# Two of the four weight sums of each seven-product step formed by accumulating DMA transfers, with six buffers for sums instead of four

## The chip, the core and the metric

The kernel runs on one core of one Trainium2 chip. The metric is the device time of one execution in microseconds (us). The core has five instruction streams that run in order, each on its own: TensorE (PE, matmuls), VectorE (DVE), ScalarE (ACT), GpSimd (POOL), and SyncE (SP), which here issues nearly all DMA transfers. They wait for one another by semaphores. An instruction that waits holds up everything behind it on its engine.

## The reference, cut to what matters

Two layers of a streaming encoder are applied to 592 tokens (16 learned meta tokens, 512 frames of a new stream, 64 frames of a running one) of width 1024:

```
def _swiglu(x, w_gate, w_up, w_down):
    return (jax.nn.silu(x @ w_gate) * (x @ w_up)) @ w_down
...
    for l in range(DEPTH):
        h = h + 0.5 * _swiglu(_rmsnorm(h, ln_ffa_w[l]), ffa_w_gate[l], ffa_w_up[l], ffa_w_down[l])
        m, c, s, g = _mixer(_rmsnorm(h, ln_mix_w[l]), ...)
        h = h + m
        h = h + 0.5 * _swiglu(_rmsnorm(h, ln_ffb_w[l]), ffb_w_gate[l], ffb_w_up[l], ffb_w_down[l])
    return _rmsnorm(h, ln_f_w), ...
```

The hidden width of each of the four feed-forward blocks (FFN) is 2816. The mixer is one input projection, a state-space scan and a gated linear attention side by side, and one output projection. All is float32. The change touches the gate and up products of the FFNs only.

## The kernel before

The activations stay in SBUF as `h`, 8 blocks of 128 features by 592 tokens. An FFN walks over 22 blocks of 128 hidden columns in four chunks (6, 6, 5 and 5 blocks). Within a chunk the gate and up products of its blocks come first, then eight down products that add into `h`.

The first two blocks of an FFN are multiplied in plain float32 (L593). Each of the other 20 is a `Quad`: the gate and the up weights of the block, each cut into an upper and a lower half of 512 rows (g1, g2, u1, u2), are replaced by seven matrices, so that seven products (in the order g1, s1, s2, s4, s3, g2, u2) do the work of eight half products. Four of the seven are sums of weights:

s1 = u1 + u2, s2 = s1 + g1, s4 = s2 + g2, s3 = g1 + u1.

Each of the seven matrices is then split by `convert` into a high part on ACT (tile `wh`, L542) and a low part on DVE (tile `wl`, L546). A product is 12 matmuls of 128x296 (L627 high by high, L628 high weights by low activations, L629 low by high). Results leave PSUM through the sink in `gated`: the sink of product s3 (L895, tile `u`) must be done before the last product, u2, may start, because they share an accumulator, and the next steps are L899, L906, L909 and L915 on DVE. So a Quad is 84 matmuls on PE, and there are 80 Quads in the program.

Weights arrive by SP, 256 KB a tile (128 partitions by 4 rows of 512 bytes), in `raw` buffers (tag `raw`, six of them, tile `wr`). The sums go into buffers with the tag `zq` (tile `ws`), which the mixers use too.

A planner fixes the order on every engine at build time: each step of the program is a generator that yields the engine and a planned duration, and the planner emits the step that could start first. The planned times only set the order; on the chip each engine takes its list from the top, and waits at its head for what is late.

Of the kernel before, what the change touches and what calls it, by code (L numbers as in the profile page):

```python
# [9 lines left out]
F32 = mybir.dt.float32  # L10
# [3 lines left out]
ALU = mybir.AluOpType  # L14
PSUM = bass.MemoryType.PSUM

P = 128
# [7 lines left out]
T = NMETA + SEQ + DEC  # L25
# [9 lines left out]


BLK = ((0, 128), (128, 128), (256, 128), (384, 128), (512, 80))
NT = 50
UK = 4
LEVELS = (64, 32, 16, 8, 4, 2, 1)  # L40

# [73 lines left out]
def ns_dve(n):  # L115
    return 67 + n / 0.96


def ns_act(n):
    return 90 + n / 1.2  # L120
# [76 lines left out]
def body(ctx: ExitStack, tc: tile.TileContext, a: dict, o: dict):  # L197
    nc = tc.nc
    V, S, G, PE, SP = nc.vector, nc.scalar, nc.gpsimd, nc.tensor, nc.sync

    const = ctx.enter_context(tc.tile_pool(name="const", bufs=1))
    res = ctx.enter_context(tc.tile_pool(name="res", bufs=1))
    sb = ctx.enter_context(tc.tile_pool(name="sb", bufs=1))
    ps = ctx.enter_context(tc.tile_pool(name="ps", bufs=1, space=PSUM))
    plan = Plan({PE: (200.0, 60.0), V: (220.0, 0.0), S: (265.0, 0.0), G: (100.0, 0.0)}, {G: V})
    bT = Buf(sb, "T", NT, [P, T], F32, 6)
    bhw = Buf(sb, "hw", 6, [P, HT], F32)
    bzq = Buf(sb, "zq", 4, [P, T], F32)
    braw = Buf(sb, "raw", 6, [P, UK, P], F32)
    bhi = Buf(sb, "whi", 6, [P, UK, P], F32R)  # L210
    blo = Buf(sb, "wlo", 6, [P, UK, P], F32R)
# [185 lines left out]
    def near(order):  # L397
        return 1e-3 * order
# [51 lines left out]
    def fetch():  # L450
# [9 lines left out]
        for i, job in enumerate(jobs):  # L460
            if isinstance(job, Quad):
                yield from fetch_quad(i, job, chain)
                continue
            src = job.src.rearrange("(k p) c -> p k c", p=P)
            for k0, k1, u in job.units:
                if job.whole:
                    if i == 0:
                        yield from whole(i, job, src, k0, k1, u, chain)
                    else:
                        plan.add(near(job.order), whole(i, job, src, k0, k1, u, chain))  # L470
                    if i == 0:
                        for b, g in ((0, 1), (1, 1), (2, 1)) if k0 == 0 else ():
                            yield from fetch_x(b, g)
                    continue
                t = yield "DMA", 190 * (k1 - k0), (), (braw,)
                raw = braw.tile(f"wr{i}", [P, k1 - k0, src.shape[2]])
                SP.dma_start(raw, src[:, k0:k1])
                t += 2000.0
                if job.few:
                    plan.add(near(job.order), convert_few(i, job, u, raw, t, chain))  # L480
                else:
                    plan.add(near(job.order), convert(u, raw, chain, braw.put, t))
            if i == 1:
                for b, g in ((3, 0), (4, 0), (3, 1), (4, 1)):
                    yield from fetch_x(b, g)
                t = yield "DMA", 380, ()
                SP.dma_start(cf[:, P:], a["c_f"][:, P:3 * P])
                cf_ev.set(t + 2000)
                load_params()
# [11 lines left out]
    def scaled(norm, k0, k1, u, t):  # L501
# [2 lines left out]
        V.tensor_tensor(u.hi[:, :u.n], u.hi[:, :u.n], w.to_broadcast([P, u.n, P]), op=ALU.mult)  # L504
        u.ready.set(t)

    def fetch_quad(i, job, chain):
        half = UK * P
        got = {}
        for name, w, r0 in (("g1", job.wg, 0), ("u1", job.wu, 0), ("u2", job.wu, half), ("g2", job.wg, half)):  # L510
            t = yield "DMA", 190 * UK, (), (braw,)
            raw = braw.tile(f"wr{i}")
            SP.dma_start(raw, w[r0:r0 + half].rearrange("(k p) c -> p k c", p=P))
            got[name] = [raw, Ev(), Ev({"g1": 3}.get(name, 2), braw.put)]
            got[name][1].set(t + 2000.0)
        for name, n in (("s1", 2), ("s2", 2), ("s4", 1), ("s3", 1)):
            got[name] = [None, Ev(), Ev(n, bzq.put)]
        plan.add(near(job.order), combine(i, got))
        for k, ((name, _, _), u) in enumerate(zip(QUAD, job.units)):
            raw, ev, use = got[name]  # L520
            plan.add(near(job.order + k), convert(u, got[name], chain, use.set, ev))

    def combine(i, got):
        for name, p, q in (("s1", "u1", "u2"), ("s2", "s1", "g1"), ("s4", "s2", "g2"), ("s3", "g1", "u1")):
            t = yield V, ns_dve(UK * P), (got[p][1], got[q][1]), (bzq,)
            dst = got[name][0] = bzq.tile(f"ws{i}", [P, UK, P])
            V.tensor_tensor(dst, got[p][0], got[q][0], op=ALU.add)  # L527
            got[name][1].set(t)
            got[p][2].set(t)
            got[q][2].set(t)  # L530

    def convert(u, raw, chain, done, *waits):

        prev, chain[0] = chain[0], Ev()
        split = chain[0]
        n = u.n * P
        t = yield S, ns_act(n), (*waits, prev) if prev else waits, (bhi,)
        if isinstance(raw, list):
            raw = raw[0]
        u.hi = bhi.tile("wh")  # L540
        hi = u.hi[:, :u.n]
        S.activation(hi, raw, AF.Copy)  # L542
        split.set(0.0)
        t = yield V, ns_dve(n), (t,), (blo,)
        u.lo = blo.tile("wl")
        V.tensor_tensor(u.lo[:, :u.n], raw, hi.bitcast(F32), op=ALU.subtract)  # L546
        done(t)
        u.ready.set(t)
# [145 lines left out]
    class Norm:  # L694
# [20 lines left out]
        def start(self):  # L715
            if self.first:
                self.first = False
                self.hi, self.lo, self.made = [None] * KD, [None] * KD, [Ev() for _ in range(KD)]
                self.rstd = res.tile([P, T], F32, tag="rstd", name=f"rs_{self.name}", bufs=2)
                plan.add(near(self.order), self.finish())  # L720

        def feed(self, m, hf, sl, *ts):
# [272 lines left out]
    for e in range(2):  # L995
        t = const.tile([P, 5 * P], F32, name=f"att{e}")
# [939 lines left out]
```

## Time and profile before

| | before |
|---|---|
| runs (us) | 2345.09, 2344.61, 2342.85 (median 2344.61) |
| profiled execution (us) | 2345.73, of which span 2343.6 |
| granted TensorE clock | 0.995 of full speed |
| busy: PE, DVE, ACT, POOL (us) | 2307.6, 1703.8, 1083.8, 122.0 |
| DMA, mean | 80 GB/s, 188 MB |

The span is the time from the first to the last instruction that the profile shows. The profiled execution is 1.1 us above the median of the runs; sums are made against the profiled one and then moved by that.

### The profile page before, as it was taken

How to read it: one execution, taken by the hardware profiler on the slowest of the kernel's cores; microseconds unless marked ns; L12 is line 12 of the kernel's file. 1: busy time of each engine (PE TensorE's matmuls, PEld its weight loads, DVE VectorE, ACT ScalarE, POOL GpSimd, SP SyncE). 2: the span in 40 equal slices, each digit the busy share in tenths (PEclk: the TensorE clock that was granted, in tenths of full speed). 3: DMA queues.
4: the chain of work that ended last, by engine and by line, in shares of the span. 5: the costliest groups of instructions: out<-in, count | busy, mean ns of one | idle time of the engine just before them, and what ended most of it. 6: DMA issues, size and time to landing. Idle time of an engine off the chain costs nothing.

```text
span 2343.6 us, 42925 instructions
## 1 busy us (share of the span) xinstructions
PE 2307.6 (98%) x16703; PEld 2243.3 (96%) x16703; DVE 1703.8 (73%) x3391; ACT 1083.8 (46%) x2155; POOL 122.0 (5%) x167
## 2 busy tenths in 40 slices
PE   8999999999999999999999999999999999999998
PEld 6999999999899899999989999999998998999998
DVE  6766767579976877576787767675789679685675
ACT  5544435446443444353534435354564534353543
POOL 0000000021300000000000000000212000000002
PEclk9999999999999999999999999999999999999999
DMA  4332332332112133323223332323211231333332
GB/s 119 95 97 82 90 91 76 97 80 54 28 52 86 41 100 90 91 76 98 81 68 95 94 92 74 101 82 92 73 43 38 60 94 51 91 89 92 91 93 75
DMA packets 370362, 188.23 MB, mean 80 GB/s; under 512 B 16672, under 2 KB 367696, under 8 KB 370160
## 3 DMA queue, kind: packets, MB, share of 16 engines
q1 hardware_dynamic: 370160, 185.50, 27.7%
q8 instruction: 131, 2.15, 0.4%
q14 instruction: 71, 0.58, 0.1%
HBM read 180.94 MB, written 4.51 MB: 79 GB/s over the span
## 4 chain that ended last, share of the span: by engine, by line
PE 83%; DVE 12%; DMA 2%; ACT 1%; issue 1%; SPq 0%; POOL 0%; DVEq 0%; ACTq 0%
PE pq L629 11%; PE pq L627 11%; PE pq L628 11%; PE pd L601 8%; PE pd L602 8%; PE pd L600 8%; DVE wl L546 2%; PE pg L593 2%; PE px L601 1%; PE px L600 1%; PE px L602 1%; PE po L600 1%; PE pa L1320 1%; PE po L601 1%; PE po L602 1%; DVE ws L527 1%
## 5 line engine op out<-in xcount | busy, mean ns | idle before, releaser
L542 ACT ACTIVATE wh<-wr 128x512 fp32r<-128x512 f32 (+2 forms) x640 | 365.4, 574 | 416.4 <-PE pd L601 242.4
L546 DVE TENSOR_TENSOR wl<-wr,wh 128x512 fp32r<-128x512 f32 (+2 forms) x640 | 388.0, 624 | 59.9 <-ACT wh L542 52.6
L600 PE MATMUL pd<-gh,wh 128*128 128x296 f32 (+3 forms) x1408 | 419.9, 298 | 2.4 <-ACT gh L913 2.4
L601 PE MATMUL pd<-gl,wh 128*128 128x296 f32 (+3 forms) x1408 | 419.8, 298 | 0.8 <-DVE gl L915 0.8
L602 PE MATMUL pd<-gh,wl 128*128 128x296 f32 (+3 forms) x1408 | 419.5, 298 | 0.0
L542 ACT ACTIVATE wh<-ws 128x512 fp32r<-128x512 f32 x320 | 201.0, 630 | 267.1 <-PE pq L628 133.2
L628 PE MATMUL pq<-ql_a,wh 128*128 128x296 f32 x960 | 287.4, 299 | 1.3 <-DVE ql_a L812 1.3
L628 PE MATMUL pq<-ql_b,wh 128*128 128x296 f32 (+1 forms) x960 | 285.8, 298 | 1.9 <-DVE ql_b L812 1.9
L627 PE MATMUL pq<-qh_a,wh 128*128 128x296 f32 x960 | 287.5, 299 | 0.1
L629 PE MATMUL pq<-qh_a,wl 128*128 128x296 f32 x960 | 286.2, 298 | 0.2
L627 PE MATMUL pq<-qh_b,wh 128*128 128x296 f32 (+1 forms) x960 | 285.3, 297 | 0.1
L629 PE MATMUL pq<-qh_b,wl 128*128 128x296 f32 (+1 forms) x960 | 284.9, 297 | 0.3 <-DVE wl L546 0.2
L600 PEld LDWEIGHTS pd<-gh,wh 128*128 128x128 f32 x1408 | 265.4, 188 | 2.9 <-ACT gh L913 2.9
L601 PEld LDWEIGHTS pd<-gl,wh 128*128 128x128 f32 x1408 | 265.5, 189 | 1.2 <-DVE gl L915 1.2
L602 PEld LDWEIGHTS pd<-gh,wl 128*128 128x128 f32 x1408 | 265.6, 189 | 0.0
L981 DVE SCALAR_TENSOR_TENSOR h<-pd,h 128x296 f32<-128x296 f32 (+3 forms) x256 | 117.7, 463 | 199.9 <-PE pd L602 198.3
L546 DVE TENSOR_TENSOR wl<-ws,wh 128x512 fp32r<-128x512 f32 x320 | 216.9, 685 | 50.0 <-ACT wh L542 47.2
L628 PEld LDWEIGHTS pq<-ql_b,wh 128*128 128x128 f32 x960 | 180.7, 188 | 4.0 <-DVE ql_b L812 3.8
L628 PEld LDWEIGHTS pq<-ql_a,wh 128*128 128x128 f32 x960 | 180.8, 188 | 3.4 <-DVE ql_a L812 3.3
L629 PEld LDWEIGHTS pq<-qh_a,wl 128*128 128x128 f32 x960 | 180.8, 188 | 0.7 <-DVE wl L546 0.7
L627 PEld LDWEIGHTS pq<-qh_b,wh 128*128 128x128 f32 x960 | 180.6, 188 | 0.8 <-ACT gg L876 0.6
L629 PEld LDWEIGHTS pq<-qh_b,wl 128*128 128x128 f32 x960 | 180.5, 188 | 0.8 <-DVE wl L546 0.8
(443 smaller groups left out, 4925.8 us busy)
## 6 DMA issues: line engine op xcount, KB each, us to landing
wr<-in_w_in SPq DMA_DIRECT2D x112, 256.0 KB, 3.1
wr<-in_ffa_w_gate SPq DMA_DIRECT2D x88, 256.0 KB, 3.1
wr<-in_ffa_w_up SPq DMA_DIRECT2D x88, 256.0 KB, 3.1
wr<-in_ffb_w_gate SPq DMA_DIRECT2D x88, 256.0 KB, 3.1
wr<-in_ffb_w_up SPq DMA_DIRECT2D x88, 256.0 KB, 3.2
wr<-in_ffa_w_down SPq DMA_DIRECT2D x96, 192.0 KB, 2.5
wr<-in_ffb_w_down SPq DMA_DIRECT2D x96, 192.0 KB, 2.6
wr<-in_w_out SPq DMA_DIRECT2D x32, 256.0 KB, 3.0
```

What stands on the lines that cost most here:

```text
L527: V.tensor_tensor(dst, got[p][0], got[q][0], op=ALU.add)
L542: S.activation(hi, raw, AF.Copy)
L546: V.tensor_tensor(u.lo[:, :u.n], raw, hi.bitcast(F32), op=ALU.subtract)
L593: PE.matmul(out[:, :n], u.hi[:, i], job.x(job.ks[j], sl), start=(j == 0), stop=(j == nk - 1))
L600: PE.matmul(out[:, :n], u.hi[:, i], xh, start=(j == 0), stop=False)
L601: PE.matmul(out[:, :n], u.hi[:, i], xl, start=False, stop=False)
L602: PE.matmul(out[:, :n], u.lo[:, i], xh, start=False, stop=(j == nk - 1))
L627: PE.matmul(out, u.hi[:, j], xh, start=(new and j == 0), stop=False, skip_group_check=True)
L628: PE.matmul(out, u.hi[:, j], xl, start=False, stop=False, skip_group_check=True)
L629: PE.matmul(out, u.lo[:, j], xh, start=False, stop=(j == UK - 1), skip_group_check=True)
L981: V.scalar_tensor_tensor(h[:, m, sl], pt, 0.5, h[:, m, sl], op0=ALU.mult, op1=ALU.add)
L1320: PE.matmul(pt[:n, c0 // 2:(c0 + n) // 2], ks[:, c0:c0 + n], qs[:, c0 // 2:(c0 + n) // 2], start=True, stop=True)
```

## The change

Two of the four sums, s1 and s3, are no longer added by DVE. SP loads u1 into a `zq` buffer as any weight tile (L528 of the changed kernel), and when that has landed POOL issues a second transfer onto the same buffer that adds u2 (for s1) or g1 (for s3) to what is there (L538). So u1 is read from memory twice and g1 and u2 twice, and u1 takes no `raw` buffer. DVE still adds s2 and s4 (L546 in the changed kernel; `convert`'s low part moves to L565, and the sinks L890, L895, L899, L906, L909, L915 move to L909, L914, L918, L925, L928, L934).

For each Quad SP issues five loads instead of four, POOL two accumulating transfers, and DVE two adds instead of four. The `zq` buffers go from 4 to 6, the buffers `T` from 50 to 49, one [128, 592] tile is kept in one copy instead of two, and the scratch space for transfers that GpSimd issues goes from 1024 to 2048. In the planner the loads of a Quad's two accumulated sums, and its two adds, follow the adds of the Quad ahead.

```
-        for name, w, r0 in (("g1", job.wg, 0), ("u1", job.wu, 0), ("u2", job.wu, half), ("g2", job.wg, half)):
-            t = yield "DMA", 190 * UK, (), (braw,)
-            raw = braw.tile(f"wr{i}")
-            SP.dma_start(raw, w[r0:r0 + half].rearrange("(k p) c -> p k c", p=P))
...
+        for name, first, second in (("s1", "u1", "u2"), ("g1", "g1", None), ("s3", "u1", "g1"), ("u2", "u2", None),
+                                    ("g2", "g2", None)):
+            buf = braw if second is None else bzq
+            t = yield "DMA", 190 * UK, () if second is None else (sums_ev[0],), (buf,)
+            raw = got[name][0] = buf.tile(f"w{name[0]}{i}", [P, UK, P])
+            SP.dma_start(raw, block(first))
+            if second is None:
+                got[name][1].set(t + 2000.0)
+            else:
+                plan.add(near(job.order), add_to(raw, block(second), got[name][1], t + 2000.0))
...
+    def add_to(raw, src, ev, t):
+        t = yield G, 1000, (t,)
+        G.dma_start(raw, src, accum_op=ALU.add)
+        ev.set(t + 4000.0)
...
-    def combine(i, got):
-        for name, p, q in (("s1", "u1", "u2"), ("s2", "s1", "g1"), ("s4", "s2", "g2"), ("s3", "g1", "u1")):
-            t = yield V, ns_dve(UK * P), (got[p][1], got[q][1]), (bzq,)
+    def combine(i, got, before, mine):
+        for name, p, q in (("s2", "s1", "g1"), ("s4", "s2", "g2")):
+            t = yield V, ns_dve(UK * P), (got[p][1], got[q][1], before), (bzq,)
```

The first place at which the order matters is the middle of a chunk, on DVE. In the kernel before, one Quad's worth of DVE's list reads so (`ws` are sums, `wl` low parts, `gg`, `u` and `gl` the sinks; the numbers only tell tiles apart):

```order
L890 TENSOR_TENSOR gg<-pq_1_1890,gg 128x296
L527 TENSOR_TENSOR ws_1963<-wr_1902,wr_1931 128x512
L546 TENSOR_TENSOR wl<-ws_1837,wh 128x512
L895 SCALAR_TENSOR_TENSOR u_1919<-pq_0_1867,u_1919 128x296
L527 TENSOR_TENSOR ws_1983<-ws_1963,wr_1886 128x512
L546 TENSOR_TENSOR wl<-ws_1856,wh 128x512
L899 TENSOR_TENSOR gg<-pq_2_1973,gg 128x296
L527 TENSOR_TENSOR ws_2002<-ws_1983,wr_1942 128x512
L546 TENSOR_TENSOR wl<-ws_1877,wh 128x512
L906 SCALAR_TENSOR_TENSOR gg<-pq_0_1867,gg 128x296
L527 TENSOR_TENSOR ws_2023<-wr_1886,wr_1902 128x512
L909 TENSOR_TENSOR gg<-u_1919,gg 128x296
```

The same stretch of DVE's list after the change:

```order
L909 TENSOR_TENSOR gg<-pq_1_1898,gg 128x296
L546 TENSOR_TENSOR ws_1967<-ws_1860,wg_1871 128x512
L565 TENSOR_TENSOR wl<-ws_1821,wh 128x512
L914 SCALAR_TENSOR_TENSOR u_1927<-pq_0_1873,u_1927 128x296
L546 TENSOR_TENSOR ws_1987<-ws_1967,wg_1931 128x512
L565 TENSOR_TENSOR wl<-ws_1841,wh 128x512
L918 TENSOR_TENSOR gg<-pq_2_1977,gg 128x296
L565 TENSOR_TENSOR wl<-ws_1737,wh 128x512
L925 SCALAR_TENSOR_TENSOR gg<-pq_0_1873,gg 128x296
L928 TENSOR_TENSOR gg<-u_1927,gg 128x296
```

The first two adds keep their places between the sinks, with an accumulated sum (`ws_1860`) as one input, and the third and fourth are gone. The next Quad's stretch, one period later, begins so:

```order
L909 TENSOR_TENSOR gg<-pq_1_2044,gg 128x296
L546 TENSOR_TENSOR ws_2115<-ws_2006,wg_2017 128x512
L565 TENSOR_TENSOR wl<-ws_1967,wh 128x512
L914 SCALAR_TENSOR_TENSOR u_2073<-pq_0_2019,u_2073 128x296
L546 TENSOR_TENSOR ws_2135<-ws_2115,wg_2077 128x512
L565 TENSOR_TENSOR wl<-ws_1987,wh 128x512
```

Its first row reads the accumulated sum `ws_2006`. The load that starts that sum takes the buffer of `ws_1841`, and so waits on SP for the row `wl<-ws_1841` of the fence above; POOL's transfer then waits for the load, and this add for POOL's transfer. In its turn the last row here, `wl<-ws_1987`, releases the load for the Quad after.

The second place is DVE's list at the start of the program, where the plain blocks' weights (`wr`, L504) are scaled and the statistics of the input (`st_x`, `sh_a`) are made. Before:

```order
L527 TENSOR_TENSOR ws_248<-wr_211,wr_218 128x512
L527 TENSOR_TENSOR ws_254<-ws_248,wr_196 128x512
L851 TENSOR_TENSOR st_x<-sx 128x5
L852 TENSOR_SCALAR st_x<-st_x 128x5
L527 TENSOR_TENSOR ws_261<-ws_254,wr_227 128x512
L527 TENSOR_TENSOR ws_266<-wr_196,wr_211 128x512
L504 TENSOR_TENSOR wr_250<-wr_250,par_a 128x512
L665 CAST sh_a_273<-st_x 128x5
```

After the change the same stretch of DVE's list reads:

```order
L870 TENSOR_TENSOR st_x<-sx 128x5
L871 TENSOR_SCALAR st_x<-st_x 128x5
L504 TENSOR_TENSOR wr_245<-wr_245,par_a 128x512
L684 CAST sh_a_271<-st_x 128x5
L685 TENSOR_TENSOR sl_a_272<-st_x,sh_a_271 128x5
L504 TENSOR_TENSOR wr_250<-wr_250,par_a 128x512
```

The four adds no longer stand ahead of the scalings; the two that remain follow eleven rows further down. On POOL the first two accumulating transfers stand ahead of the step that turns `st_x` into a reciprocal root, which `sh_a` reads.

The third place is SP's list at the first change from Quads to down products, where the mixer's small parameters are loaded. Before (`wr` are weights of the down product here):

```order
L477 DMA wr_846<-in_ffa_w_down 128x3x128
L477 DMA wr_874<-in_ffa_w_down 128x3x128
L477 DMA wr_917<-in_ffa_w_down 128x3x128
L477 DMA wr_926<-in_ffa_w_down 128x3x128
L283 DMA dtb<-in_dt_bias 8x1
...
L292 DMA reset<-in_c_reset 128x592
L477 DMA wr_1012<-in_ffa_w_down 128x3x128
```

And after the change:

```order
L528 DMA wg_764<-in_ffa_w_gate 128x4x128
L477 DMA wr_767<-in_ffa_w_down 128x3x128
L283 DMA dtb<-in_dt_bias 8x1
...
L292 DMA reset<-in_c_reset 128x592
L477 DMA wr_871<-in_ffa_w_down 128x3x128
L477 DMA wr_897<-in_ffa_w_down 128x3x128
```

The parameters follow the first weights of the down products instead of the fourth. Elsewhere PE's list within the Quads and down products is the same, and in the mixers, of layer 1 above all, some projections change places.

## Rows read from the trace of the kernel before

**Rows 1.** The page: busy time by engine, and the queue that SP's transfers use.
```profile
PE 2307.6 (98%) x16703; PEld 2243.3 (96%) x16703; DVE 1703.8 (73%) x3391; ACT 1083.8 (46%) x2155; POOL 122.0 (5%) x167
...
q1 hardware_dynamic: 370160, 185.50, 27.7%
```

**Rows 2.** Busy time by stretch: start:end, length, engines, granted clock, DMA share, GB/s.
```profile
0.00:40.00 40.00, 30.21 (x119) 22.85 (x120) 22.08 (x47) 18.32 (x40) 3.02 (x7) 0.91 0.60 167
40.00:80.00 40.00, 39.27 (x234) 34.74 (x233) 39.90 (x76) 21.62 (x43) 0.00 (x0) 1.00 0.17 50
100.00:110.00 10.00, 7.58 (x53) 7.12 (x52) 6.38 (x22) 5.86 (x10) 1.17 (x3) 0.99 0.68 203
...
1300.00:1340.00 40.00, 40.00 (x296) 40.00 (x295) 30.35 (x54) 20.44 (x37) 0.00 (x0) 1.00 0.29 83
540.00:720.00 180.00, 173.46 (x1343) 162.42 (x1342) 148.05 (x337) 88.96 (x209) 29.64 (x26) 0.98 0.17 45
1680.00:1840.00 160.00, 154.90 (x1221) 144.36 (x1221) 143.48 (x324) 88.41 (x206) 30.17 (x27) 0.99 0.17 45
```

**Rows 3.** PE's waits: what waited for what, us in all, times, longest.
```profile
PE pS L1640 <- DVE xw L1598: 6.7, 2, 3.3
...
PE pu L593 <- DVE sh_a L665: 3.9, 1, 3.9
...
PE pd L600 <- ACT gh L913: 2.4, 2, 2.0
PE pq L628 <- DVE ql_b L812: 1.9, 2, 1.2
```

**Rows 4.** DVE's adds of weights, grouped by shape: busy, mean ns, idle before.
```profile
L527 DVE TENSOR_TENSOR ws<-wr,wr 128x512 f32<-128x512 f32 x160 | 109.5, 684 | 28.3 <-DMA wr<-in_ffb_w_up 15.8 <-DMA wr<-in_ffa_w_up 11.6
L527 DVE TENSOR_TENSOR ws<-ws,wr 128x512 f32<-128x512 f32 x160 | 108.9, 681 | 0.1
```

**Rows 5.** DVE in the middle of a chunk: start, duration, instruction.
```profile
1313.41 0.47 DVE L890 TENSOR_TENSOR gg<-pq,gg 128x296 f32<-128x296 f32 x1
1313.80 0.68 DVE L527 TENSOR_TENSOR ws<-wr,wr 128x512 f32<-128x512 f32 x1
...
1315.03 0.47 DVE L895 SCALAR_TENSOR_TENSOR u<-pq,u 128x296 f32<-128x296 f32 x1
...
1316.01 0.68 DVE L546 TENSOR_TENSOR wl<-ws,wh 128x512 fp32r<-128x512 f32 x1
...
1324.85 0.47 DVE L890 TENSOR_TENSOR gg<-pq,gg 128x296 f32<-128x296 f32 x1
```

**Rows 6.** PE in the same stretch: the first matmul of the product u2.
```profile
1316.47 0.30 PE L627 MATMUL pq<-q_a,wh 128*128 128x296 f32 x1
```

**Rows 7.** Transfers: count, KB each, median us from issue to landing.
```profile
wr<-in_ffa_w_gate SPq DMA_DIRECT2D x88, 256.0 KB, 3.1
...
wr<-in_ffa_w_down SPq DMA_DIRECT2D x32, 128.0 KB, 2.3
...
reset<-in_c_reset SPq DMA_DIRECT2D x1, 296.0 KB, 10.1
```

**Rows 8.** POOL's largest group by line and shape.
```profile
L1615 POOL TENSOR_TENSOR ls<-cf,lal 128x512 fp32r<-128x512 f32 x20 | 25.3, 1267 | 6.9 <-DVE l L1200 5.6 <-PE tt L1220 0.7 <-PE py L1672 0.6
```

**Rows 9.** DVE in the first mixer, while POOL ran four of these.
```profile
592.26 4.09 DVE L1211 SCALAR_TENSOR_TENSOR cmk<-cmk,lnc,cum 128x592 f32<-128x592 f32 x1
```

**Rows 10.** DVE near the start of the program.
```profile
20.65 0.68 DVE L527 TENSOR_TENSOR ws<-ws,wr 128x512 f32<-128x512 f32 x1
...
21.86 0.68 DVE L504 TENSOR_TENSOR wr<-wr,par_a 128x512 f32<-128x512 f32 x1
22.46 0.16 DVE L665 CAST sh_a<-st_x 128x5 fp32r<-128x5 f32 x1
...
22.73 0.68 DVE L504 TENSOR_TENSOR wr<-wr,par_a 128x512 f32<-128x512 f32 x1
```

**Rows 11.** ACT at the first down products.
```profile
103.70 0.53 ACT L542 ACTIVATE wh<-wr 128x384 fp32r<-128x384 f32 x1 [0.73 <-DMA wr<-in_ffa_w_down]
```

More of the change, by code (lines that the diff above doesn't have):

```diff
@@ L37 @@
 BLK = ((0, 128), (128, 128), (256, 128), (384, 128), (512, 80))
-NT = 50
+NT = 49
 UK = 4
@@ L207, in body @@
     bhw = Buf(sb, "hw", 6, [P, HT], F32)
-    bzq = Buf(sb, "zq", 4, [P, T], F32)
+    bzq = Buf(sb, "zq", 6, [P, T], F32)
     braw = Buf(sb, "raw", 6, [P, UK, P], F32)
@@ L505, in scaled, with block @@
         u.ready.set(t)
+    sums_ev = [Ev(0)]
     def fetch_quad(i, job, chain):
         half = UK * P
+        def block(name):
+            w, r0 = {"g": job.wg, "u": job.wu}[name[0]], half * (int(name[1]) - 1)
+            return w[r0:r0 + half].rearrange("(k p) c -> p k c", p=P)
         got = {}
-        for name, w, r0 in (("g1", job.wg, 0), ("u1", job.wu, 0), ("u2", job.wu, half), ("g2", job.wg, half)):
-            t = yield "DMA", 190 * UK, (), (braw,)
-            raw = braw.tile(f"wr{i}")
-            SP.dma_start(raw, w[r0:r0 + half].rearrange("(k p) c -> p k c", p=P))
[L514 to L518, printed above, removed]
+        for name, n in (("s1", 2), ("g1", 2), ("s3", 1), ("u2", 1), ("g2", 2), ("s2", 2), ("s4", 1)):
+            got[name] = [None, Ev(), Ev(n, (bzq if name[0] == "s" else braw).put)]
+        before, mine = sums_ev[0], Ev(2)
+        plan.add(near(job.order), combine(i, got, before, mine))
         for k, ((name, _, _), u) in enumerate(zip(QUAD, job.units)):
@@ L521, in fetch_quad @@
             plan.add(near(job.order + k), convert(u, got[name], chain, use.set, ev))
-    def combine(i, got):
-        for name, p, q in (("s1", "u1", "u2"), ("s2", "s1", "g1"), ("s4", "s2", "g2"), ("s3", "g1", "u1")):
-            t = yield V, ns_dve(UK * P), (got[p][1], got[q][1]), (bzq,)
+        for name, first, second in (("s1", "u1", "u2"), ("g1", "g1", None), ("s3", "u1", "g1"), ("u2", "u2", None),
[8 more added lines that the diff above has]
+                plan.add(near(job.order), add_to(raw, block(second), got[name][1], t + 2000.0))
+        sums_ev[0] = mine
+    def add_to(raw, src, ev, t):
[5 more added lines that the diff above has]
+            t = yield V, ns_dve(UK * P), (got[p][1], got[q][1], before), (bzq,)
+            mine.set(0.0)
             dst = got[name][0] = bzq.tile(f"ws{i}", [P, UK, P])
@@ L718, in start @@
                 self.hi, self.lo, self.made = [None] * KD, [None] * KD, [Ev() for _ in range(KD)]
-                self.rstd = res.tile([P, T], F32, tag="rstd", name=f"rs_{self.name}", bufs=2)
+                self.rstd = res.tile([P, T], F32, tag="rstd", name=f"rs_{self.name}", bufs=1)
                 plan.add(near(self.order), self.finish())
@@ L1923 @@
     from concourse.bass_utils import run_bass_kernel_spmd as _run
-    nc = _bacc.Bacc("TRN2", target_bir_lowering=False, num_devices=1, dynamic_dma_scratch_size=1024)
+    nc = _bacc.Bacc("TRN2", target_bir_lowering=False, num_devices=1, dynamic_dma_scratch_size=2048)
     arrays, a, o = {}, {}, {}
```

## The prediction

> **What bounds the kernel now.** I read the page's busy times first. PE is busy for 2307.6 of 2343.6 us, DVE for 1703.8, and POOL for 122.0 [rows 1]. So PE is the bound, and an edit elsewhere can only win back what PE stands idle, about 36 us, or make PE wait where it doesn't wait now. The second view is the stretches, to see where these 36 us lie. In a stretch of Quads and down products, 1300 to 1340, PE is busy for 40.00 of 40.00 while DVE has 9.65 us to spare [rows 2]. In the first 40 us PE is idle for 9.8 us, from 40 to 80 for 0.7, from 100 to 110 for 2.4, and in the two mixer stretches for 6.5 and 5.1. The third view, PE's waits, names what it waits for there: the largest are in the mixer (6.7 on `xw`), at the start (3.9, by name on `sh_a`), at the first down products (2.4 on `gh`) and where an FFN's first Quads wait for activations (1.9 on `ql_b`) [rows 3]. None is an add of weights. The first add of a Quad already waits 28.3 us in all at the head of DVE's list for plain loads [rows 4], and PE loses nothing by it.
>
> **What is removed.** DVE loses 160 adds of about 0.684 us, 109.5 us of busy time [rows 4]. In the steady stretches, where most of these stand, that is worth nothing, since PE is full there. The gain is looked for where PE waits:
>
> - Start. Before, two adds began at 20.65 and 21.25 and the scaling of the plain weights at 21.86; PE began the up product at 22.68, after 3.9 us of waiting [rows 3, 10]. Without the two adds the scaling can begin 21.86 - 20.65 = 1.21 us earlier, if its own load has landed. Transfers are crowded there (share 0.60 of the first 40 us [rows 2]), and POOL's root of `st_x` comes behind two transfers, so I take 0.7 of it (bounds: 1.2 gained, 1.5 lost; the second half of the scaled weights at 22.73 is the next to be late).
> - 40 to 80. DVE is busy for 39.90 of 40 us and PE idle for 0.7 [rows 2]. Several adds go: I take all of it, 0.7.
> - First down products. ACT waited 0.73 us for a weight of the down product at 103.70 [rows 11], because the load of it stood behind the parameters, of which the largest took 10.1 us to land [rows 7]. After the change the parameters go out behind the first such weight, more than a Quad earlier. PE lost 2.4 us by its busy time; by its matmuls, 53 in 10 us where the steady stretch has 296 in 40 us, thus 74, it lost (74 - 53) / 7.4 = 2.8 us [rows 2]. I take 2.8 (bounds 0 and 4).
> - The first Quads of the later FFNs, where `ql_b` is late by 1.9 us in all [rows 3] and DVE has two adds less: I take 1.0 (bounds 0 and 1.9).
> - The mixers: some projections change places, and the sums' buffers, which the mixer uses too, are six. PE's idle time of 6.5 and 5.1 us there [rows 2] can go either way; I take 0, with 3 us on both sides. POOL's transfers stand between its own steps there, but the loads that they wait for have been issued long before.
>
> **What is added.** Five loads and two accumulating transfers for a Quad instead of four loads. The kernel before has no accumulating transfer and no transfer on POOL's queue in a Quad, so its cost is bounded from rows. First the load on the transfer engines: in the steady stretch their share is 0.29 with four loads a Quad and what the next chunk fetches [rows 2]. If an accumulating transfer costs as much as a load, 0.29 x 7/4 = 0.51; if twice, because it reads its target too, 0.29 x 9/4 = 0.65; only at four times would it be 0.29 x 13/4 = 0.94. So the engines hold it.
>
> **The new wait** is the add s2 on DVE, which needs the accumulated s1 and has the sink of product s3 two rows behind it, for which PE's product u2 waits. The loop is the one that the order shows: low part of s4 of one Quad, then SP's load into its buffer, then POOL's transfer, then the add s2 one period later, then the low part of the next s4. By the rows of before, in the same places, the low part of s4 begins at 1316.01 and ends 0.68 later, at 1316.69, the period is 1324.85 - 1313.41 = 11.44, and the add can begin 0.39 behind the first sink, at 1325.24 [rows 5]. The chain of load and accumulation, call it L, has thus 1325.24 - 1316.69 = **8.55 us**. There is a cushion: the sink of s3 runs from 1315.03 to 1315.50, and the product u2 begins at 1316.47 [rows 5, 6], so 0.97 us of lateness is free. But it is free once for each chunk, as a late add makes the next release late too: if L is above 8.55, each turn of the loop is late by L - 8.55, and what is above 0.97 in a chunk is lost. Chunks have 4, 6, 5 and 5 Quads, and the loop closes from a chunk's third Quad on: 2 + 4 + 3 + 3 = 12 turns an FFN, 48 in all, in 16 chunks. The loss is 48 x (L - 8.55) - 16 x 0.97 us, from about L = 8.9 on.
>
> Now L. The plain load takes 3.1 us from issue to landing [rows 7]. POOL's part, forming the transfer, has no row; its nearest is a 128x512 operation of POOL's own, 1.27 us [rows 8], and from below nothing at all; I take 1.0, since even small steps of POOL's are of that order (the page has 122.0 us for 167 instructions, 0.7 each [rows 1]). The accumulation itself lands in 3.1 us if it is a load like others. If it moves the target's bytes as well: from 128 to 256 KB a landing goes from 2.3 to 3.1 [rows 7], 0.8 for 128 KB, so 256 KB more are 1.6, and it lands in 4.7. L lies between 3.1 + 0 + 3.1 = 6.2 and 3.1 + 1.27 + 4.7 = 9.1. I take the middle for the landing, 3.9, so L = 3.1 + 1.0 + 3.9 = **8.0 us**, under 8.55 by half a microsecond: no loss. A landing as slow as that of `reset`, 10.1 us [rows 7], would make L 14, but that was on a crowded queue (share 0.68 from 100 to 110 [rows 2]).
>
> The Trainium skill's page "DMA: Bandwidth & Descriptors", section "Anatomy of one DMA — SWDGE (gpsimd) path", gives such a transfer 2.0 us and its bytes by 436 GB/s, an estimate of 2.6 us for 256 KB; by it L would be 3.1 + 1.0 + 2.6 = 6.7, and the sum is the same.
>
> **Sum.** 0.7 + 0.7 + 2.8 + 1.0 = 5.2 us less: 2345.73 - 5.2 = 2340.5 for an execution like the profiled one, which stands 1.1 us above the median of the runs: 2339.4, say 2339.
>
> **Rivals.**
>
> - *The sums land late.* For it: the upper bound of L lies above 8.55, the load is one of seven instead of four, and nothing else in the loop can give. Against it: the rows next to an accumulation are the plain loads. At L = 9.5 it costs 48 x 0.95 - 16 x 0.97 = 30 us: 2339 + 30 = **2369**. At L = 10 it is 54 us, 2393. It decides at L = 8.9, and at 9.0 it has eaten the gain.
> - *POOL and DVE hold each other up.* A DVE operation on 592 columns took 4.09 us under four of POOL's, where DVE's 512 columns take 0.68 [rows 4, 9]. If forming a transfer holds DVE, or DVE's adds hold POOL, each transfer costs up to 1.27 us [rows 8] in the loop, L = 9.3, and 48 x 0.75 - 16 x 0.97 = 20 us: 2359. Against it: those were operations on data, 128x512 each, and forming a transfer touches no data. The page "SBUF — State Buffer" of the Trainium skill, section "Who interferes with whom", says that an operation of GpSimd and one of DVE in a two-port mode, or with two SBUF inputs against a GpSimd operation that reads SBUF, exclude each other. No row here shows it for a transfer.
> - *No change that can be told.* Transfers hide the start's gain, the parameters only move the wait, and the mixers lose 2 or 3 us: 2343. For it: the terms are small and each is next to another wait.
>
> **How the numbers follow.** What a measurement of this kernel can tell from no change is about 0.2%, 4.7 us. Chances: forecast, 0.44 (no loss in the loop 0.6, and the gain above 4.7 us in three of four of these); sums late 0.29; POOL and DVE 0.05; no change 0.22, with a small gain or a gain eaten. Thus faster 0.44, same 0.22, slower 0.34. The range begins at 2331, where every term is at its better bound and the mixers give 3 us (2339 - 0.5 - 1.2 - 0.9 - 3 is 2333, and 2 us for what I don't see), and reaches to 2393, L = 10, which leaves out some 0.12 above and 0.05 below. Of the forecast alone the range is 2332 to 2344.
>
> **What would show it.** In the steady stretch after the change PE busy for all of its time and DVE's busy time down by 1.37 us a Quad; the add s2 waiting little at the head of DVE's list; POOL's transfers landing within 4.7 us of their issue; PE's wait for `sh_a` shorter by a microsecond, and none on `gh` near 105. If the sums are late, the row is PE waiting for `u` at product u2, or for low parts, in the third to sixth Quad of a chunk, and DVE waiting for a POOL transfer at the add s2. If the parameters don't matter, the stretch 100 to 110 still has 2.4 us idle. A change of more than 3 us within a mixer would make the sum wrong without touching its reasons.

## The result, and the profile after

The changed kernel takes 2417.8 us (median of four runs, 2414.0 to 2427.2) against 2344.9 us for the kernel before on the same chip: a ratio of 1.032, with a 95% interval of 1.028 to 1.035. It is slower by 73 us, and outside the range that was given. The rival "the sums land late" came about, at a larger size than it was given: 73 us, where at most 54 was put on it.

The page of the profiled execution (2414.2 us, span 2412.4) first: busy times, the queues (packets, MB, share of 16 engines' span; q1 is SP's, q0 POOL's), and the chain that ended last.

```profile
PE 2329.2 (97%) x16703; PEld 2255.7 (94%) x16703; DVE 1608.6 (67%) x3228; ACT 1082.4 (45%) x2158; POOL 331.0 (14%) x327
...
q1 hardware_dynamic: 412400, 206.48, 30.4%
q0 software_dynamic: 84480, 41.95, 14.2%
...
PE 63%; DVE 15%; DMA 14%; issue 5%; ACT 2%; SPq 1%; POOL 0%; DVEq 0%; POOLq 0%; ACTq 0%
```

DVE is busy for 95 us less than in [rows 1] (the adds that went have 109.5 us by their own durations, which overlap a little with their neighbours'), and PE now stands idle for 83 us instead of 36. 14% of the chain that ended last are transfers. PE's waits say on whom (what waited for what, us in all, times, longest):

```profile
PE pq L646 <- DVE u L914: 40.2, 33, 3.4
PE pq L646 <- ACT gg L895: 7.0, 5, 1.9
PE pu L612 <- DVE wr L504: 6.7, 2, 4.0
```

The first row was named in advance as the mark of late sums: product u2 waits for the sink of s3, which stands on DVE behind the add s2. All 33 of these waits lie in the first four Quads of a chunk, behind the first chunk of an FFN. On DVE the group of the adds has the wait itself, 188.3 us in 160 adds, most of it for transfers:

```profile
L546 DVE TENSOR_TENSOR ws<-ws,wg 128x512 f32<-128x512 f32 x160 | 109.9, 687 | 188.3 <-DMA ws<-in_ffb_w_up 67.3 <-DMA ws<-in_ffa_w_up 62.3 <-issue 32.8
```

Where the time went is seen in stretches of one chunk each (columns as in [rows 2]): the four Quads of the first chunk, its down products, the six Quads of the second chunk, and those of the same chunk in a later FFN.

```profile
56.52:109.73 53.21, 48.22 (x338) 46.24 (x337) 42.17 (x92) 31.17 (x61) 6.52 (x8) 1.00 0.52 120
109.73:149.04 39.31, 39.31 (x291) 39.31 (x289) 17.84 (x37) 9.65 (x17) 5.20 (x4) 1.00 0.54 120
149.04:224.63 75.59, 71.39 (x506) 70.41 (x505) 48.72 (x86) 38.45 (x71) 10.35 (x8) 0.98 0.58 126
1342.85:1416.36 73.51, 69.70 (x506) 68.77 (x505) 48.50 (x85) 38.19 (x71) 10.38 (x8) 1.00 0.58 128
```

The same stretches of the kernel before:

```profile
53.75:101.70 47.95, 47.22 (x338) 45.97 (x337) 43.27 (x92) 29.03 (x57) 0.20 (x1) 1.00 0.27 79
101.70:145.26 43.56, 41.13 (x290) 40.68 (x289) 22.63 (x46) 12.14 (x22) 1.17 (x3) 0.96 0.34 99
145.26:213.75 68.49, 68.49 (x507) 68.49 (x505) 53.72 (x94) 38.66 (x71) 0.00 (x0) 1.00 0.31 91
1306.67:1375.38 68.71, 68.71 (x507) 68.65 (x506) 53.65 (x94) 38.24 (x71) 0.00 (x0) 1.00 0.31 91
```

Summed over all 16 chunks in this way, the Quads take 989.7 us instead of 921.0, 68.7 more. The first Quad begins 2.8 later, the first down products take 4.3 less, and all the rest together is 1.6 more: 68.7 + 2.8 - 4.3 + 1.6 = 68.8, the difference of the spans. So the loss of the Quads is as large as the whole. 59.0 of it lie in the 12 chunks behind an FFN's first, and 9.6 in the four first chunks, where PE waits for `gg` and not for `u`.

The chain of waits through a chunk of the third FFN shows the loop that was foretold, link by link (start, duration, what):

```profile
1341.54 4.09 DMA ws<-in_ffa_w_up
1345.63 0.02 issue
1345.65 0.04 POOLq L538
1345.70 0.61 issue
1346.30 4.71 DMA ws<-in_ffa_w_up
1351.01 0.04 DVEq L546
1351.04 0.04 issue
1351.09 0.17 DVE ws L546
...
1353.27 0.69 DVE wl L565
...
1353.99 4.27 DMA ws<-in_ffa_w_up
1358.26 0.02 issue
1358.28 0.04 POOLq L538
1358.32 0.61 issue
1358.93 4.95 DMA ws<-in_ffa_w_up
...
1363.96 0.13 DVE ws L546
```

The low part of s4 ends at 1353.96, SP's load is issued at once and lands 4.27 us later, POOL starts 0.67 us after that, its transfer lands 4.95 us after its start, and the add s2 begins at 1363.96. L is 10.0 us here, and 9.6 in the turn ahead of it. The period is 1363.96 - 1351.09 = 12.87 us; the prediction's relation, 11.44 + (10.0 - 8.55), gives 12.89. In the 12 chunks behind an FFN's first there are 40 such turns from a chunk's second Quad on; by the starts of the adds s2 they last 11.6 to 14.7 us, at the median 12.5, and L is 9.7 at the median.

### The profile page after: what moved, and what is told of

It is laid out like the page before. It is cut to its first block, busy times and chain, and to the rows that moved or that the text cites. A ratio compares the mean times of both kernels' runs of the same rounds, so it can differ in the third digit from the quotient of the medians.

```text
span 2412.4 us, 43194 instructions
## 1 busy us (share of the span) xinstructions
PE 2329.2 (97%) x16703; PEld 2255.7 (94%) x16703; DVE 1608.6 (67%) x3228; ACT 1082.4 (45%) x2158; POOL 331.0 (14%) x327
## 3 DMA queue, kind: packets, MB, share of 16 engines
q0 software_dynamic: 84480, 41.95, 14.2%
## 4 chain that ended last, share of the span: by engine, by line
PE 63%; DVE 15%; DMA 14%; issue 5%; ACT 2%; SPq 1%; POOL 0%; DVEq 0%; POOLq 0%; ACTq 0%
DMA ws<-in_ffb_w_up 7%; PE pq L646 7%; PE pq L647 6%; PE pq L648 6%; PE pd L619 6%; PE pd L620 6%; PE pd L621 6%; DMA ws<-in_ffa_w_up 5%; DVE wl L565 4%; PE px L619 1%; PE px L620 1%; PE px L621 1%; PE po L620 1%; PE po L619 1%; PE po L621 1%
## 5 line engine op out<-in xcount | busy, mean ns | idle before, releaser
L561 ACT ACTIVATE wh<-wr 128x384 fp32r<-128x384 f32 (+2 forms) x400 | 215.5, 544 | 362.9 <-PE pd L620 202.8
L565 DVE TENSOR_TENSOR wl<-ws,wh 128x512 fp32r<-128x512 f32 x320 | 217.1, 685 | 52.2 <-ACT wh L561 48.6
L565 DVE TENSOR_TENSOR wl<-wr,wh 128x384 fp32r<-128x384 f32 (+2 forms) x400 | 229.7, 602 | 30.9 <-ACT wh L561 30.0
L546 DVE TENSOR_TENSOR ws<-ws,wg 128x512 f32<-128x512 f32 x160 | 109.9, 687 | 188.3 <-DMA ws<-in_ffb_w_up 67.3
L646 PEld LDWEIGHTS pq<-qh_a,wh 128*128 128x128 f32 x960 | 182.1, 190 | 7.2 <-ACT gg L895 5.6
```

The lines of the kernel that those rows point to most:

```text
L646: PE.matmul(out, u.hi[:, j], xh, start=(new and j == 0), stop=False, skip_group_check=True)
```

## Experiments

Every version was timed on the same chip as runs of the kernel before, and stands in a ratio to them. Where a version is set beside the changed kernel, the two medians are of different chips, on which the kernel before took 2344.7 to 2346.9 us, so such differences hold to some 2 us. Lengths of single Quads below are differences of the starts of their first matmuls in the trace.

**s1 in buffers of its own.** The changed kernel, but the loop is opened: s1 has two buffers, the other sums four.

```
-    bzq = Buf(sb, "zq", 6, [P, T], F32)
+    bzq = Buf(sb, "zq", 4, [P, T], F32)
+    bs1 = Buf(sb, "s1", 2, [P, UK, P], F32)
...
-            buf = braw if second is None else bzq
+            buf = braw if second is None else bs1 if name == "s1" else bzq
```

> The changed kernel with the accumulated s1 in two buffers of its own and four zq buffers for the rest, so that the load that starts an s1 is released by the low part of the s1 two Quads before, which PE paces, and no longer by that of the last s4. All transfers stay as in the changed kernel (seven for a Quad, two of them accumulating). Theory A, the chain from s4's low part over load and accumulation to the add s2 is what costs: the Quads from a chunk's third on go back from 12 to 14 us to 11.4, and of the 73 us some 50 go, leaving 2355 to 2370. Rival B, the transfers as such are too slow (transfer engines shared by seven transfers, or POOL's queue): PE still waits, in the same number of Quads, and the time stays above 2400.

Measured: 2364.9 us, ratio 1.008 (1.006 to 1.010). Of 73 us, 53 are gone, with as many transfers as before. The six Quads of the second chunk of every FFN are back at 11.4 us each (11.1 in the last), and PE's wait for the sink is down from 33 to 6 times:

```profile
PE pq L647 <- DVE u L915: 12.1, 6, 4.8
PE pq L647 <- ACT gg L896: 7.1, 4, 2.1
```

So the loop through s4's buffer is the main cause. Transfers as such are not: POOL's queue moved the same bytes, and from the issue of the load to the landing of the sum these 40 sums even took 12.7 us at the median, where they took 9.6 in the changed kernel. With the load issued early enough, PE waits for the sink only four times behind the FFNs' first chunks. What stays is in the start, and in the first Quads of chunks.

**s3 alone by transfer.** s1 is added by DVE; the list of sums in `combine` begins with s1 again, and the load list reads

```
+        for name, first, second in (("g1", "g1", None), ("u1", "u1", None), ("u2", "u2", None), ("s3", "u1", "g1"),
+                                    ("g2", "g2", None)):
```

> Only s3 is accumulated by transfers, s1 is added by DVE again (three adds for a Quad, six transfers). s3 feeds no other sum, it is only converted, late in the Quad. Theory A: no add waits for an accumulation, so PE loses nothing in the middle of a chunk: 2338 to 2350. Rival B, accumulating transfers slow the plain loads that everything waits for: half of the loss stays, 2370 to 2390.

Measured: 2348.3 us, ratio 1.0006 (0.9997 to 1.0016), no change that can be told. PE doesn't wait for the sink at all, and DVE's adds with one input that is a sum wait 2.1 us in all. An accumulated sum that nothing adds to costs the Quads nothing in all: they take 919.8 us, where they took 921.0. The 2.9 us by which its first Quad is late is the start's, below.

**s1 alone by transfer.** The mirror: s3 is added by DVE.

```
-                                    ("s3", "u1", "g1"), ("u2", "u2", None),
+                                    ("u1", "u1", None), ("u2", "u2", None),
...
-        for name, p, q in (("s2", "s1", "g1"), ("s4", "s2", "g2")):
+        for name, p, q in (("s2", "s1", "g1"), ("s4", "s2", "g2"), ("s3", "g1", "u1")):
```

> The mirror of the kernel with s3 alone: s1 alone is accumulated by a transfer, s3 is added by DVE again, six zq buffers, scratch 2048. The loop from the low part of s4 over s1's load and accumulation to the add s2 is the same as in the changed kernel, but no other accumulating transfer stands on POOL's queue, and six transfers a Quad run instead of seven. Theory A, the loop itself is too long for its 8.55 us (load 3.5, 0.65 and the transfer 4.9 from POOL's start: 9.0): losses stay, 0.3 to 0.6 us a turn: 2350 to 2370. Rival C', the two accumulating transfers waiting for each other are the whole loss: no loss in the loop, 2342 to 2349.

Measured: 2395.6 us, ratio 1.022 (1.021 to 1.024): well over what was expected, but on theory A's side. PE waits for the sink 36.6 us in 33 times with a single accumulating transfer for a Quad, so two transfers standing in each other's way are not the whole loss. The same 40 turns last 11.5 to 14.7 us, at the median 12.5: 1.1 us too long, where 0.3 to 0.6 was expected. The long Quads are the first or second of the chunks behind an FFN's first (13 to 17 us in most of them), because DVE's list has the add s2 of a Quad two Quads ahead of PE's work on it. So the loop's turn to a chunk's third Quad makes PE wait in the first, as in the longest wait of this kernel, which belongs to a chunk that begins at 255.7:

```profile
245.15 7.80 DMA ws<-in_ffa_w_up
252.97 0.69 DVE ws L546
...
256.24 3.18 DMA ws<-in_ffa_w_up
...
260.09 6.00 DMA ws<-in_ffa_w_up
...
269.05 0.39 DVE u L914
...
269.48 0.61 PE pq L646
```

The sum that lands at 252.97 is the second Quad's, issued while PE was still at down products, and the one of 260.09 is the third Quad's. In all, the turns beyond 11.4 us (11.1 in the last FFN), less the cushion of 0.97 a chunk, make 43 us, of 49 that the 12 chunks lose.

**A plain copy in place of the accumulation.** One word, and the sums are not formed:

```
-        G.dma_start(raw, src, accum_op=ALU.add)
+        G.dma_start(raw, src)
```

> The changed kernel with POOL's second transfer as a plain copy onto the buffer: the sums s1 and s3 are left out (they hold the second addend alone), all else, POOL's queue and the waits too, is the same. It tells the price of accumulating from that of a transfer that POOL issues. Theory A1, reading the target as well is what makes the landing long: the chain falls from 9.9 to under 8.9 us and most of the loss in the loop goes, 2350 to 2370. A2, POOL's own time (0.65 us before it starts and 1.3 us of forming) and the crowded plain load are the surplus: the chain stays near 9.5, and the time at 2395 to 2415.

Measured: 2342.5 us, ratio 0.998 (0.997 to 0.999). It falls below both theories' numbers: no Quad outside the first chunk of an FFN is longer than 11.5 us. The queue that POOL feeds, and POOL's groups of transfers (the last one is the changed kernel's for the same line), say what accumulating costs:

```profile
q0 software_dynamic: 12800, 41.95, 6.0%
...
L538 POOL DMA_DIRECT2D ws<-in_ffa_w_up x40 | 30.3, 758 | 597.2 <-DVE wl L565 325.5 <-DVE h L1000 65.2 <-DVE ql_a L831 62.0
```

```profile
L538 POOL DMA_DIRECT2D ws<-in_ffa_w_up x40 | 52.1, 1303 | 511.2 <-DVE wl L565 265.6 <-DVE h L1000 91.6 <-DVE ql_a L831 63.2
```

For the same bytes, POOL forms a plain copy in 0.76 us and an accumulating one in 1.30; the copy is 12800 / 160 = 80 packets and 6.0% of the engines' span, the accumulation 84480 / 160 = 528 packets and 14.2%. From POOL's start to landing the medians over 160 transfers are 4.0 and 4.9 us. From the load's issue to POOL's landing the 40 sums take 7.6 us at the median instead of 9.6, under the 8.55 that the loop allows. In this version 66 of 159 transfers also start before the one ahead has landed, and none does in the changed kernel, so part of the difference is that (see the larger scratch below).

**Buffers alone.** The kernel before with the changed kernel's four numbers.

```
-NT = 50
+NT = 49
...
-    bzq = Buf(sb, "zq", 4, [P, T], F32)
+    bzq = Buf(sb, "zq", 6, [P, T], F32)
```

> The kernel before with the changed kernel's numbers alone: six zq buffers, 49 T buffers, one copy of the tile instead of two, the larger scratch. No transfer accumulates. Theory A: within 3 us of before, 2342 to 2348, since the Quads are full in both. Rival: the mixers' order, which the buffers change, is part of the loss: 2350 or more.

Measured: 2345.2 us, ratio 0.9997 (0.9988 to 1.0007). The buffers, and the order in the mixers that they bring, are no part of the loss.

**More room for descriptors.** In the changed kernel POOL's transfers stand in a row. None starts before the one ahead has landed, and 89 of 159 start within 0.35 us behind that landing, as here:

```profile
1346.30 1.30 POOL L538 DMA_DIRECT2D ws<-in_ffa_w_up  x1 [5.91 <-DMA ws<-in_ffa_w_up]
1351.32 1.29 POOL L538 DMA_DIRECT2D ws<-in_ffa_w_gate  x1 [3.71 <-issue]
```

The first of these landed at 1351.01 by the chain above. One number, and no instruction changes its place:

```
-dynamic_dma_scratch_size=2048)
+dynamic_dma_scratch_size=3072)
```

> The changed kernel with a larger scratch for transfers that GpSimd issues, 3072 instead of 2048, nothing else (the order of instructions is the same). In the changed kernel no accumulating transfer starts before the one ahead of it has landed (0 of 159), and its nearest follower starts 0.26 us behind the landing; where the same transfers are plain copies, 66 of 159 start earlier. Theory C, the scratch holds the descriptors of one accumulating transfer but not of two, and POOL waits for room: now starts ahead of the landing appear, the start of the program, where POOL's root of st_x stood behind two such transfers, gets 3 us back, and the loop's chain shrinks where s1 follows s3: 2380 to 2410. Rival D, accumulating transfers are serial by themselves: still 0 of 159, and 2414 to 2427 as the changed kernel.

Measured: 2385.0 us, ratio 1.016 (1.015 to 1.018): 33 us are back. Now 83 of 159 transfers start before the one ahead of them has landed, as here, where the first lands at 1345.40:

```profile
1338.92 1.30 POOL L538 DMA_DIRECT2D ws<-in_ffa_w_up  x1 [9.09 <-DVE gl L934]
1340.81 1.29 POOL L538 DMA_DIRECT2D ws<-in_ffa_w_gate  x1 [0.58 <-issue]
```

So rival D falls, and the signs that theory C named came: the size of the scratch decides whether they overlap. That it is room for descriptors is the reading of it; no run shows the scratch itself. The first Quad begins at 53.1 us instead of 56.5. But the loop stays too long, with Quads of 12 to 13 us, some longer: from start to landing a transfer takes 5.6 us instead of 4.9. That two in flight lengthen each other isn't shown, since with s1 alone, where none overlaps, the medians are 5.5 and 5.7.

**Both.** s1 in its own buffers and the scratch at 3072.

> The kernel with s1 in two buffers of its own (2364.9 us), with the scratch at 3072. It has 20 us left over the kernel before, in the program's start and in the first two Quads of chunks. Theory C (room in the scratch): transfers overlap, and the start's 5 us and part of the first Quads' come back: 2345 to 2355. Rival D (serial by themselves): 2361 to 2369, unchanged.

Measured: 2354.6 us, ratio 1.004 (1.003 to 1.006), of four runs between 2347 and 2358. In the trace, of a run of 2347.2 us, all Quads outside the first chunks of the FFNs take 11.4 us (11.1 in the last FFN); in those, one or two Quads take 12 to 15.

**A first version meant to beat both.** s3 alone by transfer, and none in the program's first chunk.

```
+        late = i > 7
...
+            if name == "s3" and not late:
+                continue
```

> A version meant to beat both: s3 alone is accumulated by a transfer, and not in the first chunk of the program, whose four Quads have their four adds on DVE. So the start, where an accumulation held POOL's root of st_x and the first activations (3 us), and the first chunk are as before, while the parameters' loads still go out early (4 us less at the first down products), and a later FFN's second Quad has 0.3 us less to wait. If these explain what the kernel with s3 alone lost and won: 2338 to 2342, 0.1 to 0.3% under before. If not: 2344 to 2350.

Measured: 2347.9 us, ratio 1.0007 (0.9998 to 1.0015). A miss. The start is as before, and the first down products take 4 us less, but the fourth Quad takes 15.3 us instead of 11.4. By its place in the trace it is the parameters' work that now stands there: ACT has three table loads among it (1.28 us each, two shown), and PE waits 2.1 us for ACT's `gg`:

```profile
90.13 1.28 ACT L323 ACT_TABLE_LOAD   x1
93.03 1.28 ACT L926 ACT_TABLE_LOAD   x1
```

```profile
PE pq L651 <- ACT gg L900: 2.1, 1, 2.1
```

**A second one.** s1 in its own buffers, scratch 3072, and in the first chunk of each FFN all four adds on DVE.

```
+        late = int(job.name[1:-1]) >= 6
...
+        for name, p, q in (("s1", "u1", "u2"), ("s2", "s1", "g1"), ("s4", "s2", "g2"), ("s3", "g1", "u1"))[1 if late else 0:3 if late else 4]:
```

In the rows beyond this cut the first-chunk Quads keep the loads of the kernel before, and a late Quad adds s2 and s4 only.

> A second version meant to beat both: s1 in two buffers of its own, scratch 3072, and the first chunk of each FFN with all four adds on DVE, since the version without that still loses 3 to 4 us in each FFN's first four Quads and none in the other chunks. If that is all that is left: the first chunks go back to 47.9 us, of 2354.6 us some 8 go, and as the mixers and the start are near before, 2340 to 2347. Below 2340 would mean a gain that I have not found; above 2350 that the accumulating transfers cost something outside the first chunks.

Measured: 2339.7 us (2337.9 to 2341.0) beside 2344.7 for the kernel before: ratio 0.998 (0.997 to 0.999). It beats both kernels, by 5.0 and by 78 us. Its second chunk, first and third FFN, with 128 transfers in the whole program:

```profile
144.39:212.87 68.48, 68.48 (x506) 68.48 (x505) 49.19 (x85) 39.01 (x71) 9.03 (x7) 1.00 0.59 129
1300.62:1369.24 68.62, 68.62 (x506) 68.62 (x505) 49.21 (x85) 38.88 (x71) 9.04 (x7) 1.00 0.58 128
```

PE is busy throughout, with DVE busy for 49 us of each, where it had 54. None of the gain is in these stretches. The time is 0.3 us below the range that was expected, and by another way: the first chunks of the later FFNs are near the 47.9 us that were named (47.8, 47.8 and 48.6), but the program's first takes 52.3. By stages it begins the first Quad 0.8 us earlier, takes 2.2 less from the last Quad of the first FFN to the first of the second, and 2.6 less in the Quads behind the program's first chunk; the first chunk and its down products together are as before. But the kernel with the buffers alone, whose time is that of the kernel before, differs from it by as much in the last two of these stages (1.7 and 2.9 us less in its trace). So the 5.0 us are measured, and where they come from stays open.

## Why the prediction was wrong, point by point

**The bound, and where a gain could lie: right.** PE was full in the Quads before, and no kernel here is faster in them than 11.4 us (11.1 in the last FFN).

**The loop, its 8.55 us and its cushion: right in form.** The place (add s2, sink of s3, product u2), the period and the releases are in the chain above, and opening the loop takes 53 us away. With plain copies, at 7.6 us, the loop costs nothing, which bears the 8.55 out. The mark was put two Quads too late: PE's waits were foretold for the third to sixth Quad of a chunk and lie in the first to fourth, as the adds run two Quads ahead of PE.

**L: the step that failed.** It was put at 8.0 us with an upper bound of 9.1, and measured 9.6 and 10.0 in the chain above, 9.7 at the median of 40 turns. So the loop didn't close in its 8.55 us, and "no loss" failed. Link by link in that chain: the plain load was 3.1 and is 4.1 to 4.3; POOL's part was 1.0 and is 0.67 from landing to start and 1.30 of forming, 1.97; the landing behind the forming was 3.9 and is 4.95 - 1.30 = 3.65. So the landing, on which most of the words were spent, came near; it was the middle of two bounds, so that is in part luck. The surplus is the load, 1.1 us, and POOL, 1.0 us. The load's price was taken from the kernel before [rows 7], whose steady Quads have a share of 0.29 on the transfer engines [rows 2]; the new stretch has 0.58, between the 0.51 and 0.65 that were worked out and then not carried into that price. That the share is what lengthens the load isn't shown: with the larger scratch it was 0.58 in the same chunk, and the loads onto the sums' buffers had medians of 3.4 and 3.7 us instead of 4.2 and 4.0. POOL's part was one duration, and the time between a landing and POOL's start, 0.67 us, was left out without a reason.

**The size of the loss.** By the prediction's relation, L = 10.0 costs 48 x 1.45 - 16 x 0.97 = 54 us; the Quads lost 68.7. The relation counts the loop alone. It has no place for the second effect, that an accumulating transfer starts only when the one ahead has landed. The larger scratch alone takes 33 us away and the open loop alone 53; they overlap, as both together take 63. With the 40 turns as they came (median 12.5 us) the relation gives 41 us of the 59 in the chunks behind an FFN's first, and 43 of 49 with s1 alone. The rest isn't singled out. One place for it is ahead of the turns that were counted: the sums of a chunk's first two Quads, issued while PE is at down products, had an L of 10.7 and 11.9 us at the median in the changed kernel. The 9.6 us of the FFNs' first chunks belong to other waits; 5.3 of them are the program's first chunk, which loses 4.4 without any transfer in it too (the two versions meant to beat both; see the parameters below).

**Start.** 0.7 us of gain was forecast with a loss of up to 1.5, and 2.8 were lost. The place was named: POOL's root of `st_x` behind two transfers. DVE's list (first fence) and POOL's (second) show it:

```profile
21.07 0.69 DVE L504 TENSOR_TENSOR wr<-wr,par_a 128x512 f32<-128x512 f32 x1 [1.51 <-DMA wr<-in_ffa_w_up]
27.27 0.17 DVE L684 CAST sh_a<-st_x 128x5 fp32r<-128x5 f32 x1 [5.50 <-POOL st_x L873]
...
27.55 0.69 DVE L504 TENSOR_TENSOR wr<-wr,par_a 128x512 f32<-128x512 f32 x1
```

```profile
17.20 1.47 POOL L538 DMA_DIRECT2D ws<-in_ffa_w_up  x1 [15.19 <-DMA ws<-in_ffa_w_up]
24.61 1.32 POOL L538 DMA_DIRECT2D ws<-in_ffa_w_gate  x1 [5.94 <-DMA rows_b<-in_ln_ffb_w]
25.48 1.75 POOL L873 TENSOR_TENSOR st_x<-st_x,mhalf 128x5 f32<-128x5 f32 x1
```

The first half of the scaled weights did begin 0.8 us earlier, at 21.07 instead of 21.86 [rows 10]. The second transfer waited on POOL for the first, which took over 7 us in the crowded start (a share of 0.87 in the first 40 us, where it was 0.60), the root for the second, and the second scaling came at 27.55 instead of 22.73. With the larger scratch the first Quad begins at 53.1, so the loss is gone; whether the 0.7 us of gain came can't be told, since the kernel before has 53.75 and the one with the buffers alone 54.95.

**First down products.** The wait for `gh` is gone, and with 4.3 us the gain there is more than the 2.8 forecast. But the first chunk's Quads pay it back: in the version without any transfer in that chunk its Quads take 52.3 us instead of 48.0. The kernel with the buffers alone, which keeps the parameters' old place, takes 48.1. The parameters' work on ACT and DVE now falls into those Quads. That it is this work is read from its place in the trace; no run tested it alone. So the term of 2.8 us was moved and not won.

**40 to 80, the first Quads of later FFNs, the mixers.** The second Quad of each FFN takes 11.4 to 11.5 us instead of 11.8 (11.2 instead of 11.6 in the last), 0.3 to 0.5 us each, so DVE's relief is real: 1.2 us in the three later FFNs, against 1.0, and 0.3 in the first, against the 0.7 for 40 to 80. The mixers move by less than 2 us, as allowed for.

**The rival of POOL and DVE.** Not seen: DVE's adds take 687 ns beside 681 and 684 [rows 4], and POOL, where nothing else holds it, starts 0.67 us behind the landing of the load (DVE was busy at 120 of its 160 starts). The rule of the Trainium skill, "SBUF — State Buffer", "Who interferes with whom", has no effect here that a row shows.

**The estimate from the Trainium skill.** Its page "DMA: Bandwidth & Descriptors", "Anatomy of one DMA — SWDGE (gpsimd) path", gave an estimate of 2.6 us for 256 KB. Here a plain copy of POOL's lands 4.0 us after its start, 0.76 of it forming, and an accumulation 4.9, 1.30 of it forming. The measurement decides.

## What to carry to other kernels

A busy engine that isn't the bound costs nothing, and here moving its work to a transfer put a latency of some 10 us (load, pick-up, forming, accumulation) where a load of 3 us and 0.7 us of an operation stood. Before such a move, find the loop that the buffer closes, and price every link as it is in the crowded stretch after the change, not in the quiet one before. If the accumulated tile only feeds a late conversion, or its buffer is released by what the bound engine paces, the steady stretches paid nothing here (s3 alone, and s1 in buffers of its own), and then a gain can only be where the relieved engine held the bound up.

## What the runs showed of the hardware that was not expected

- With a scratch of 2048 no accumulating transfer of 128 x 4 rows of 512 bytes started before the one ahead had landed (0 of 159); with 3072, 83 of 159 did. Plain copies of the same tiles did so with 2048 (66 of 159).
- An accumulating transfer of 256 KB was 528 packets, a plain copy by POOL 80, and per MB POOL's queue took 14.2 / 41.95 = 0.34% of the engines' span accumulating and 0.14% copying, beside 0.15% of SP's loads.
- POOL started 0.67 us (median) after the landing that it waited for.
